# Linear attention that scales keys and queries by doubling block totals

## The chip, the cores and the metric

One core of one Trainium2 chip. The metric is device time in microseconds of one execution; less is better. The kernel computes two transformer blocks on 512 tokens of width 1024, in f32. Most products run on operands split in two fp32r parts (high and low), three products for one; the linear attention's inner products run on plain f32.

## The reference

Block 1 (two layers of feed-forward, pooling or convolution, feed-forward) and, in block 2, the softmax attention, the merge and the MLP are not touched. The change lies in block 2's gated linear attention: 4 heads, key width 128, value width 256, 512 tokens and 256 context tokens, run forward and backward. Cut to what matters:

```python
g = log_sigmoid(lowrank @ w_gk + b_gk) / 16            # per token and key channel, one for either direction
s_f = sum_t k_t * exp(b_last - b_t) v_t                # b = cumsum(g) over the context; s_b likewise, flipped
# in chunks of 64, state S from s_f:
b = cumsum(gc)
o_inter = (qc * exp(b)) @ state
a[i, j] = sum_d qc[i, d] kc[j, d] exp(b[i, d] - b[j, d])   for j <= i
o = o_inter + a @ vc
state = exp(b_last) * state + (kc * exp(b_last - b)).T @ vc
# the same on flipped time; the two outputs are added, normalized and gated
```

## The kernel before

Data lie transposed: channels on the 128 partitions, tokens along the free dimension. For one head H, `H.k` holds keys of 512 tokens and 256 context tokens, `H.q` the queries, `H.v` the values with tokens on partitions. The kernel works in chunks of 128 tokens.

The matrix of a chunk is built by halving. At level s (64, 32, ..., 1) a chunk falls in blocks of 2s tokens; each pair of a token in the left half and one in the right half of one block is decayed across the block's middle: the key by what lies from it to the middle, the query by what lies from the middle to it. In the right half's queries against the left half's keys this is the forward direction; in the left half's queries against the right half's keys the backward one. `masks` pick these pairs from a product of all keys and queries (`copy_predicated` into `H.A`), and the diagonal comes from undecayed keys and queries, times 2.

The decays come from TensorE. `decay` computes the log decays of 4 chunks (f32 products of the gate inputs `lr`, tokens as the stationary side, with `gkw`; then Abs, Exp, Ln, a VectorE step, and a split in Gh and Gl). For each direction there are 9 constant patterns of 128 x 128 (`pats`): a state's key, a state's query, and 7 levels. `gla_decays` multiplies two patterns at a time with Gl and Gh (L940, L941), and ScalarE takes the exponential of the sums into E (L942). `gla_level` multiplies halves of keys and queries by E into X and Y (L962), multiplies X by Y on TensorE (L966), and writes through the mask (L968). For the first pair of patterns `gla_states` instead scales keys (kd) and queries (qp), transposes the keys (`ktok`), and runs `state_step`: a product of transposed keys with values, and S times a chunk's total plus the product. `gla_ctx_keys` and `gla_ctx_states` do that for the context. `gla_final` adds the state's part in both directions and `H.A` times values.

The order: `gla_phase` goes through the heads. Between a head's pairs of patterns it places "fills": the next head's projections (keys, values, queries; after the last head the attention's keys), the head's two output gates, and some gates of the later merge; the next head's decays (`begin`) stand between them as well. The program order is only a priority: the framework's planner simulates the program with its own costs and gives every engine one fixed order, in which a ready instruction may pass one that isn't. Engines then run in that order and wait on semaphores. Weights come as 512 KB chunks over SyncE's queue into 3 raw slots; ScalarE casts each into a high part (L199), VectorE subtracts (L200), with 2 slots of either part. Sums in PSUM have 4 slots for this work ("mm") and 2 for projections ("pj").

The lines to follow: L204 to L206 are the three products of a projection, L871 to L873 those of the values, L782 the gate products, L838 the diagonal products, L879 the state products, L891 the transposes, L905 and L906 the context's pattern products.

Of the kernel before, what the change touches and what calls it, by code (L numbers as in the profile page):

```python
# [17 lines left out]
P = 128  # L18
# [14 lines left out]
LEVELS = (64, 32, 16, 8, 4, 2, 1)  # L33
NPAT = 2 + len(LEVELS)
GLA_FILLS = (0, 2, 1, 2, 3)
# [15 lines left out]
def consts():  # L51
# [10 lines left out]
    u = np.arange(P)[:, None]  # L62
    t = np.arange(P)[None, :]
    pats = np.zeros((2, NPAT, P, P), np.float32)
    masks = np.zeros((len(LEVELS), P, P), np.float32)
    for d in range(2):
        pats[d, 0] = (u > t) if d == 0 else (u < t)
        pats[d, 1] = (u <= t) if d == 0 else (u >= t)
        for n, s in enumerate(LEVELS):
            mid = (t // (2 * s)) * 2 * s + s  # L70
            left = t < mid
            if d == 0:
                key, query = (u > t) & (u < mid), (u >= mid) & (u <= t)
                pats[d, 2 + n] = np.where(left, key, query)
            else:
                query, key = (u >= t) & (u < mid), (u >= mid) & (u < t)
                pats[d, 2 + n] = np.where(left, query, key)
            j, i = u, t
            same = (j // (2 * s)) == (i // (2 * s))
            jl, il = (j % (2 * s)) < s, (i % (2 * s)) < s  # L80
            masks[n] = same & (jl != il)
    out["pats"] = np.ascontiguousarray(pats.transpose(2, 0, 1, 3) * GSCALE).reshape(P, 2 * NPAT * P).astype(np.float32)
# [18 lines left out]
def layout(inp):  # L101
# [47 lines left out]
    gw[0:16, 0], gw[64, 0] = a["w_gk_fwd_2"][0], a["b_gk_fwd_2"][0]  # L149
    gw[16:32, 1], gw[64, 1] = a["w_gk_bwd_2"][0], a["b_gk_bwd_2"][0]  # L150
# [15 lines left out]
class Builder:  # L166
# [165 lines left out]
    def out_rows(self, load, xs, gate, slots=()):  # L332
        """tail(seg, acc): x += gate * (W^T xs) and its sums of squares, the last rows by segments."""
# [326 lines left out]
    def gla_phase(self, ctx, gla):  # L660
# [3 lines left out]
        self.pe = self.pool(ctx, "glae", 1, reuse_waits="tile")  # L664
        self.pz = self.pool(ctx, "glaz", 2, reuse_waits="tile")
        self.lr = cp.tile([P, T + C], F32, name="lrT")
        nc.gpsimd.memset(self.lr, 1.0)
        H = self.gla_open(0, gla)
        self.first_values(H)
        npat = NPAT * P  # L670
        self.pats = [cp.tile([P, npat], F32R, name=f"pats{i}") for i in range(2)]
        for i in range(2):
            for s in range(0, npat, 576):
                raw = self.raw(d["pats"][:, i * npat + s:i * npat + s + 576], 576)
                nc.scalar.copy(self.pats[i][:, s:s + 576], raw)
# [4 lines left out]
        self.gkw = cp.tile([P, 2, 512], F32, name="gkw")  # L680
        nc.sync.dma_start(self.gkw, d["gkw"])
        self.eye2 = cp.tile([P, P], F32, name="eye2")
        nc.vector.tensor_scalar(self.eye2, self.ident, 2.0, None, ALU.mult)
        parts, begin = self.gla_proj(H), self.gla_begin(H)
        for step in (begin[0], parts[0], begin[1], parts[4], begin[3], begin[4]):
            step()
        for hd in range(GH):
            N = self.gla_open(hd + 1, gla) if hd + 1 < GH else None
            fills = self.gla_proj(N) if N else self.k_proj()
            fills += [lambda H=H, e=e: self.gla_gate(H, e) for e in range(2)]  # L690
            if hd == 0:
                fills += [lambda: self.merge_gates(1) for _ in range(1)]
            if not N:
                fills += [lambda: self.merge_gates(1) for i in range(3)]
            begin = self.gla_begin(N) if N else []
            self.gla_init(H)
            for n, p0 in enumerate(range(0, NPAT, 2)):
                E = self.gla_decays(H, p0)
                if n == 4 and N:
                    begin[4]()  # L700
                self.gla_level(H, p0, E)
                for f in fills[:GLA_FILLS[n]]:
                    f()
                fills = fills[GLA_FILLS[n]:]
                if N and n < 4:
                    begin[n]()
            self.gla_final(H)
            H = N

    def first_values(self, H):  # L710
        """The first head's values and, in the same products, the low-rank gate inputs of all heads."""
        nc = self.nc
        own = tuple(self.pe.tile([P, 1024], F32R, name=f"wv{i}", tag=f"E{i}", bufs=2) for i in range(2))
# [8 lines left out]
        for tts in ((4, 5), (0, 1), (2, 3)):  # L722
# [5 lines left out]
            nc.scalar.copy(self.lr[0:32, at:at + n], ps[0:32, :n])  # L728

    def gla_begin(self, H):  # L730
        H.G = [None, None]

        def direction(dr):
            H.G[dr] = self.decay(H.hd, [(dr, c * P) for c in range(4)])

        def context():
            H.Gc = self.decay(H.hd, [(b, T + c * P) for b in range(2) for c in range(2)])

        def states():
            direction(0)  # L740
            self.gla_ctx_states(H)

        return [context, lambda: self.gla_ctx_keys(H), lambda: None, states, lambda: direction(1)]
# [34 lines left out]
    def decay(self, hd, parts):  # L778
        nc = self.nc
        ps = self.psum()  # L780
        for n, (b, at) in enumerate(parts):
            nc.tensor.matmul(ps[:, n * P:(n + 1) * P], self.lr[:, at:at + P], self.gkw[:, b, hd * P:(hd + 1) * P],  # L782
                             start=True, stop=True)
        e = self.ptmp.tile([P, T], F32, name="ge", tag="sa")
        nc.scalar.activation(e, ps, AF.Abs)
        nc.scalar.activation(e, e, AF.Exp, scale=-1.0)
        nc.scalar.activation(e, e, AF.Ln, bias=1.0)
        nc.vector.scalar_tensor_tensor(e, ps, 0.0, e, ALU.min, ALU.subtract)
        hi = self.pz.tile([P, T], F32R, name="Gh", tag="Gh", bufs=3)
        lo = self.pz.tile([P, T], F32R, name="Gl", tag="Gl", bufs=3)  # L790
        self.split(hi, lo, e)
        return hi, lo

    def gla_open(self, hd, gla):
        H = SimpleNamespace(hd=hd, out=gla[2 * hd:2 * hd + 2])
        H.k = self.pk.tile([P, T + C], F32, name="kT", bufs=2)
# [4 lines left out]
    def gla_proj(self, H):  # L801
# [3 lines left out]
        def keys():  # L805
            w = self.wm(WM_G + 2 * H.hd)
            for xs, at, n in ((self.hcs, T, C), (self.hs, 0, T)):
                ps = self.psum("pj")
                self.proj(ps[:, :n], w, xs)
                nc.scalar.copy(H.k[:, at:at + n], ps[:, :n])  # L810
# [21 lines left out]
    def gla_init(self, H):  # L832
        nc = self.nc
        H.A = self.pz.tile([P, 4, P], F32, name="glaA", tag="glaA", bufs=2)
        ps = self.psum()
        for c in range(4):
            s = slice(c * P, (c + 1) * P)
            nc.tensor.matmul(ps[:, s], H.k[:, s], H.q[:, s], start=True, stop=True)  # L838
        nc.vector.tensor_tensor(H.A, ps.rearrange("p (c t) -> p c t", c=4), self.eye2.unsqueeze(1).to_broadcast([P, 4, P]), ALU.mult)
# [47 lines left out]
    def ktok(self, kd, n):  # L887
        nc = self.nc
        ps = self.psum()
        for c in range(n):  # L890
            nc.tensor.transpose(ps[:, c * P:(c + 1) * P], kd[:, c * P:(c + 1) * P], self.ident)  # L891
        kt = self.pz.tile([P, T], F32, name="ktok", tag="ktok")
        nc.scalar.copy(kt[:, :n * P], ps[:, :n * P])
        return kt

    def gla_ctx_keys(self, H):
        nc = self.nc
        gh, gl = H.Gc
        H.ctx = []
        for dr in range(2):  # L900
            ps = self.psum()
            for c in range(2):
                o = ps[:, c * 256:(c + 1) * 256]
                s = slice((dr * 2 + c) * P, (dr * 2 + c + 1) * P)
                nc.tensor.matmul(o, gl[:, s], self.pats[dr][:, 0:256], start=True, stop=False)  # L905
                nc.tensor.matmul(o, gh[:, s], self.pats[dr][:, 0:256], start=False, stop=True)  # L906
            E = self.pe.tile([P, 2, 2, P], F32, name="Ec", tag=f"E{dr}", bufs=2)
            nc.scalar.activation(E.rearrange("p c s t -> p (c s t)"), ps, AF.Exp)
            kd = self.pz.tile([P, T], F32, name="kd", tag="X")
            nc.vector.tensor_tensor(kd[:, :C].rearrange("p (c t) -> p c t", c=2), H.k[:, T:].rearrange("p (c t) -> p c t", c=2),  # L910
# [319 lines left out]
```

## Time and profile before

| what | value |
|---|---|
| timed runs, median of 3 | 2787.91 us (2782.96 to 2790.6) |
| the profiled execution, span | 2789.4 us (its own time is not given apart from the span) |
| TensorE products busy | 2749.3 us, 99% |
| VectorE, ScalarE, GpSimd busy | 1534.0, 973.7, 30.7 us |
| linear attention | about 1700 to 2054 us of the span |

Busy times add up what an engine's instructions cover. A product's own duration reaches to the end of its pipeline, so products overlap: their throughput is read from one start to the next. One f32 product on TensorE leaves two records, one in fp32r leaves one, a transpose one. What ended an idle time is inferred from semaphore events.

### The profile page before, as it was taken

To read this page: it belongs to the slowest core of one execution; us is meant where nothing else is said; L and a number is where in the kernel's file an instruction comes from. 1 tells how busy PE (TensorE), PEld (TensorE's weight loads), DVE (VectorE), ACT (ScalarE), POOL (GpSimd) and SP (SyncE) were. 2 spreads that over 40 slices of the span, in tenths; PEclk is the share of its full clock that TensorE was granted. 3 is DMA by queue.
4 is the path that set the end of the run, shared out by engine and by line. 5 is a ranking of instruction groups with operands and counts; after the bars stand their busy time and mean duration, and the time that the engine had idled before them with its cause. 6 is when DMAs were issued, how large, how long until landed. Compare 5 with 4: busy or idle time off the path is not lost.

```text
span 2789.4 us, 35584 instructions
## 1 busy us (share of the span) xinstructions
PE 2749.3 (99%) x14437; PEld 2374.9 (85%) x14437; DVE 1534.0 (55%) x2553; ACT 973.7 (35%) x1509; POOL 30.7 (1%) x39
## 2 busy tenths in 40 slices
PE   7999999999999999999999999999999999999999
PEld 6888889888898888988988889999898888888887
DVE  6645577444575446744865545455456665454443
ACT  4222244222242222322432234444456652333222
POOL 0000000000000000000000000000000000000000
PEclk9999999999999999999999999999999999999999
DMA  8745543444545455332455433111121134323332
GB/s 313 249 147 184 190 128 129 144 145 132 161 134 184 153 164 171 107 100 91 154 185 163 154 103 121 54 35 39 46 80 53 57 109 145 97 92 93 103 95 81
DMA packets 102980, 354.60 MB, mean 127 GB/s; under 512 B 11424, under 2 KB 11680, under 8 KB 102688
## 3 DMA queue, kind: packets, MB, share of 16 engines
q1 hardware_dynamic: 100800, 348.66, 39.5%
q10 hardware_dynamic: 2016, 3.67, 0.3%
q8 instruction: 113, 1.85, 0.3%
q14 instruction: 51, 0.42, 0.0%
HBM read 344.42 MB, written 7.86 MB: 126 GB/s over the span
## 4 chain that ended last, share of the span: by engine, by line
PE 96%; ACT 1%; DVE 1%; DMA 1%; issue 0%; POOL 0%; SPq 0%; DVEq 0%; ACTq 0%
PE mm L204 28%; PE mm L206 28%; PE mm L205 28%; PE mm L871 1%; PE mm L872 1%; PE mm L873 1%; PE mm L966 1%; PE mm L1078 1%; PE mm L879 1%; PE mm L941 1%; PE mm L940 1%; ACT whi L199 0%; PE mm L458 0%; PE mm L504 0%; PE nR L285 0%
## 5 line engine op out<-in xcount | busy, mean ns | idle before, releaser
L204 PE MATMUL mm<-hh,wlo 128*128 128x512 f32 (+1 forms) x2344 | 881.1, 378 | 2.8 <-ACT hh L301 1.8
L205 PE MATMUL mm<-hh,whi 128*128 128x512 f32 (+1 forms) x2344 | 878.9, 377 | 0.0
L206 PE MATMUL mm<-hl,whi 128*128 128x512 f32 (+1 forms) x2344 | 870.0, 377 | 0.4 <-DVE hl L302 0.3
L199 ACT CAST whi<-wraw 128x1024 fp32r<-128x1024 f32 (+1 forms) x443 | 457.0, 1034 | 904.8 <-PE mm L206 484.9
L200 DVE TENSOR_TENSOR wlo<-wraw,whi 128x1024 fp32r<-128x1024 f32 (+1 forms) x443 | 533.0, 1205 | 314.4 <-ACT whi L199 312.0
L204 PEld LDWEIGHTS mm<-hh,wlo 128*128 128x128 f32 x2344 | 442.8, 189 | 81.2 <-ACT hh L301 2.2
L205 PEld LDWEIGHTS mm<-hh,whi 128*128 128x128 f32 x2344 | 442.4, 189 | 77.6
L206 PEld LDWEIGHTS mm<-hl,whi 128*128 128x128 f32 x2344 | 437.5, 189 | 80.2 <-DVE hl L302 0.8
L205 PE MATMUL mm<-g,whi 128*128 128x512 f32 (+1 forms) x1147 | 416.2, 363 | 0.0
L204 PE MATMUL mm<-g,wlo 128*128 128x512 f32 (+1 forms) x1147 | 416.0, 363 | 0.0
L206 PE MATMUL mm<-g,whi 128*128 128x512 f32 (+1 forms) x1147 | 413.7, 362 | 0.0
L205 PEld LDWEIGHTS mm<-g,whi 128*128 128x128 f32 x1147 | 216.5, 189 | 33.5
L206 PEld LDWEIGHTS mm<-g,whi 128*128 128x128 f32 x1147 | 216.5, 189 | 33.5
L204 PEld LDWEIGHTS mm<-g,wlo 128*128 128x128 f32 x1147 | 216.5, 189 | 33.4
L249 DVE SCALAR_TENSOR_TENSOR adaw<-adaw,cond 128x1024 f32<-128x1024 f32 x176 | 208.7, 1220 | 2.5 <-DMA adaw<-in_ada_dram 2.5
L324 DVE SCALAR_TENSOR_TENSOR x<-mm,hg,x 128x512 f32<-128x512 f32 (+1 forms) x115 | 76.2, 662 | 186.2 <-PE mm L206 186.2
L363 DVE TENSOR_TENSOR gf<-sa,mm 128x512 f32<-128x512 f32 (+1 forms) x94 | 61.3, 653 | 200.4 <-PE mm L206 191.8
L362 ACT ACTIVATE sa<-mm 128x512 f32<-128x512 f32 (+1 forms) x94 | 53.6, 570 | 316.2 <-PE mm L206 316.2
L324 DVE SCALAR_TENSOR_TENSOR x<-mm,mod,x 128x512 f32<-128x512 f32 (+1 forms) x56 | 37.8, 674 | 134.1 <-PE mm L206 134.1
L301 ACT ACTIVATE hh<-hn,mod 128x256 fp32r<-128x256 f32 (+1 forms) x120 | 58.4, 519 | 58.5 <-DVE hn L300 49.5
L269 DVE TENSOR_TENSOR nacc<-nacc,sq 128x256 f32<-128x256 f32 (+1 forms) x108 | 52.2, 486 | 27.7 <-ACT sq L268 27.2
L268 ACT ACTIVATE sq<-x 128x256 f32<-128x256 f32 (+1 forms) x90 | 42.1, 468 | 67.7 <-DVE x L324 64.2
(283 smaller groups left out, 2812.7 us busy)
## 6 DMA issues: line engine op xcount, KB each, us to landing
wraw<-in_ffn_in_dram SPq DMA_DIRECT2D x176, 512.0 KB, 3.6
adaw<-in_ada_dram SPq DMA_DIRECT2D x176, 512.0 KB, 4.6
wraw<-in_wm_dram SPq DMA_DIRECT2D x66, 512.0 KB, 3.6
wraw<-in_mlp_dram SPq DMA_DIRECT2D x64, 512.0 KB, 3.9
wraw<-in_ffn_out_dram SPq DMA_DIRECT2D x64, 448.0 KB, 3.4
wraw<-in_ffn_out_dram SPq DMA_DIRECT2D x32, 512.0 KB, 3.6
wraw<-in_conv_in_dram SPq DMA_DIRECT2D x24, 512.0 KB, 3.5
ads<-in_ada_dram SPq DMA_DIRECT2D x8, 512.0 KB, 10.0
```

The costliest lines, as they stand in the source:

```text
L199: self.nc.scalar.copy(hi, src)
L200: return self.nc.vector.tensor_tensor(lo, src, hi.bitcast(F32), ALU.subtract)
L204: mm(ps, wlo, xhi, start=start, stop=False)
L205: mm(ps, whi, xhi, start=False, stop=False)
L206: mm(ps, whi, xlo, start=False, stop=stop)
L249: nc.vector.scalar_tensor_tensor(out, raw, 1.0, self.cond[:, cond], ALU.mult, ALU.mult, accum_out=dst)
L268: nc.scalar.activation(sq[:, :n], src, AF.Square, scale=g)
L269: nc.vector.tensor_tensor(acc, acc, sq[:, :n], ALU.add)
L301: nc.scalar.activation(hi, u, AF.Identity, bias=sh[:, k:k + 1])
L324: self.nc.vector.scalar_tensor_tensor(x, ps[:, :seg[1]], gate[:, k:k + 1], x, ALU.mult, ALU.add)
L362: nc.scalar.activation(sa, pa[:, :seg[1]], AF.Silu)
L363: nc.vector.tensor_tensor(gf, sa, pb[:, :seg[1]], ALU.mult)
```

## The change

The patterns, their products and their exponentials go, and with them the tiles E, Y, Gh and Gl. Decays now are products of decays. `H.tot` starts as each token's own decay in either direction (forward of context and tokens, backward of tokens and context; 1536 columns). Two stacked tiles, L = [context keys, keys, backward queries] and R = [forward queries, keys, context keys], hold keys and queries decayed to the borders of their block. One level with blocks of s tokens: X takes the left half-block keys of L and the right ones of R; the product with queries of both stacks (read with a two-step pattern from Z, which holds L and R) goes through the mask; then the left halves of L and the right halves of R are multiplied by the total of the other half, and totals are multiplied in pairs. Levels run from 1 to 64, each on the result of the one before; after the last, keys and queries are decayed to borders of a chunk, and the states follow (`gla_states`), now behind all levels, context included.

The gate: inputs, their remainders and the inputs again stand in rows 0 to 95 of `lr`, rounded to fp32r, the bias in rows 96 and 97; `gate_weights` prepares the stacked weights once (cast, remainder, cast, and two steps for rows 96 on). One product per direction and 512 columns then gives the gate. The number of fills and of merge gates is as before; their places between levels are new.

```diff
-LEVELS = (64, 32, 16, 8, 4, 2, 1)
+LEVELS = (1, 2, 4, 8, 16, 32, 64)
@@ gla_phase
-        self.pats = [cp.tile([P, npat], F32R, name=f"pats{i}") for i in range(2)]
-                raw = self.raw(d["pats"][:, i * npat + s:i * npat + s + 576], 576)
-                nc.scalar.copy(self.pats[i][:, s:s + 576], raw)
+        self.gate_weights(cp)
-        for step in (begin[0], parts[0], begin[1], parts[4], begin[3], begin[4]):
+        for step in (parts[0], lambda: self.gla_decay(H), parts[4], lambda: self.gla_enter(H)):
             step()
...
+                fills = [[p[0]], [p[4], lambda N=N: self.gla_decay(N)], [p[1]], [p[2]], [p[3], lambda N=N: self.gla_enter(N)]]
+                fills += [[g] for g in gates]
+            else:
+                fills = [[k[0]], [k[1]], [gates[0]], [gates[1]]] + [[m] for m in more]
+            for n in range(len(LEVELS)):
+                self.gla_level(H, n)
+                for f in fills[n]:
                     f()
+            self.gla_states(H)
             self.gla_final(H)
+    def gate_weights(self, cp):
+        self.gkw = cp.tile([P, 1024], F32R, name="gkw")
+        raw = self.raw(self.d["gkw"], 1024)
+        lo = self.wraw.tile([P, 1024], F32, name="gklo", tag="wraw")
+        hi = self.gkw.bitcast(F32)
+        nc.scalar.copy(self.gkw, raw)
+        nc.vector.tensor_tensor(lo[64:P], raw[64:P], hi[64:P], ALU.subtract)
+        nc.scalar.copy(self.gkw[64:96], lo[64:96])
+        nc.vector.tensor_scalar(raw[96:P], hi[96:P], self.ident[96:P, 96:97], None, ALU.mult)
+        nc.vector.scalar_tensor_tensor(self.gkw[96:P], lo[96:P], self.ident[96:P, 97:98], raw[96:P], ALU.mult, ALU.add)
@@ first_values, for each pair of token tiles
+            nc.scalar.copy(self.lr[0:32, s], ps[0:32, :n])
+            nc.vector.tensor_tensor(self.lr[32:64, s], ps[0:32, :n], self.lr[0:32, s].bitcast(F32), ALU.subtract)
+            nc.scalar.copy(self.lr[64:96, s], ps[0:32, :n])
+    def gla_decay(self, H):
+        groups = (((0, 0, T, C),), ((1, 0, T, T + C),), ((0, T, C, 0), (1, T, C, 2 * T + C)))
+        for group in groups:
+            for dr, t0, n, _ in group:
+                w = self.gkw[:, dr * T + H.hd * P:dr * T + (H.hd + 1) * P]
+                nc.tensor.matmul(ps[:, at:at + n], w, self.lr[:, t0:t0 + n], start=True, stop=True)
...
+        nc.scalar.activation(H.tot, H.tot, AF.Exp, scale=GSCALE)
+    def gla_enter(self, H):
+        nc.vector.tensor_tensor(H.L[:, T + C:], H.q, H.tot[:, T + C:2 * T + C], ALU.mult)
+        nc.vector.tensor_tensor(H.R[:, :T], H.q, H.tot[:, C:T + C], ALU.mult)
...
@@ keys of gla_proj
+                nc.scalar.copy(H.L[:, left:left + n], ps[:, :n])
+                nc.gpsimd.tensor_copy(H.R[:, right:right + n], H.L[:, left:left + n])
+    def gla_level(self, H, n):
+        nc.scalar.copy(blocks(X)[:, :, 0], blocks(H.L[:, C:C + T])[:, :, 0])
+        nc.scalar.copy(blocks(X)[:, :, 1], blocks(H.R[:, T:2 * T])[:, :, 1])
+        for c in range(4):
+            q = H.Z[:, T + C + c * P:T + C + (c + 1) * P]
+            dims = [[2 * s, P // (2 * s)], [T + s, 2], [1, s]]
+            q = bass.AP(q.tensor, q.offset, [list(q.ap[0])] + [x for x in dims if x[1] > 1])
+            nc.tensor.matmul(ps[:, t], X[:, t], q, start=True, stop=True)
+        nc.vector.copy_predicated(H.A, m, ps.rearrange("p (c t) -> p c t", c=4))
+        w = (2 * T + C) // s
+        for a, h, tot in ((H.L, 0, H.tot[:, :w]), (H.R, 1, H.tot[:, C // s:C // s + w])):
+            a = blocks(a)[:, :, h]
+            other = tot.rearrange("p (b h) -> p b h", h=2)[:, :, 1 - h]
+            nc.vector.tensor_tensor(a, a, other.unsqueeze(2).to_broadcast([P, w // 2, s]), ALU.mult)
+        pairs = H.tot.rearrange("p (b h) -> p b h", h=2)
+        nc.vector.tensor_tensor(H.tot, pairs[:, :, 0], pairs[:, :, 1], ALU.mult)   # a new tile
+    def gla_states(self, H):
+        kc = self.ktok([L[:, :P], L[:, P:C], R[:, 2 * T:2 * T + P], R[:, 2 * T + P:]])
+        kts = [self.ktok([a[:, c * P:(c + 1) * P] for c in range(4)]) for a in (L[:, C:C + T], R[:, T:2 * T])]
...
+        H.qp = [R[:, :T], L[:, T + C:]]
```

## Rows read from the trace of the kernel before

**Rows 1.** The page, parts 1 and 2: busy time of each engine; granted clock of 40 slices.
```profile
PE 2749.3 (99%) x14437; PEld 2374.9 (85%) x14437; DVE 1534.0 (55%) x2553; ACT 973.7 (35%) x1509; POOL 30.7 (1%) x39
...
PEclk9999999999999999999999999999999999999999
```

**Rows 2.** Busy time by stretch: stretch, us, then each engine's busy us (instructions).
```profile
1690.00:1740.00 50.00, 46.38 (x335) 43.82 (x334) 28.73 (x64) 27.11 (x60) 1.06 (x2) 1.00 0.47 152
...
sum 370.00, PE 362.63 PEld 334.12 DVE 182.19 ACT 167.89 POOL 4.08; mean PE 72.53 PEld 66.82 DVE 36.44 ACT 33.58 POOL 0.82
```

**Rows 3.** What TensorE waited for, 1690 to 2060 us: total, times, longest.
```profile
PE mm L966 <- DVE X L962: 2.6, 2, 1.6
...
PE mm L879 <- ACT ktok L893: 0.7, 3, 0.2
```

**Rows 4.** Groups by line and shape, TensorE, 1690 to 2065: count | busy, mean ns | idle.
```profile
L940 PE MATMUL mm<-pats,Gl 128*128 128x256 f32 x128 | 33.7, 295 | 0.1
...
L966 PE MATMUL mm<-Y,X 128*128 128x128 f32 x224 | 27.9, 276 | 2.6 <-DVE X L962 2.6
...
L782 PE MATMUL mm<-gkw,lrT 128*128 128x128 f32 x96 | 12.8, 276 | 0.0
...
L940 PE MATMUL mm<-pats,Gl 128*128 128x128 f32 x32 | 7.3, 273 | 0.0
...
L905 PE MATMUL mm<-pats,Gl 128*128 128x256 f32 x16 | 4.7, 309 | 0.0
```

**Rows 5.** Timeline of TensorE, 1747 to 1761: start us, us, instruction.
```profile
1747.60 0.39 PE L204 MATMUL mm<-hh,wlo 128*128 128x512 f32 x1
...
1749.86 0.39 PE L205 MATMUL mm<-hh,whi 128*128 128x512 f32 x1
...
1759.67 0.28 PE L940 MATMUL mm<-pats,Gl 128*128 128x256 f32 x1
...
1760.62 0.28 PE L873 MATMUL mm<-wlo,hc 128*128 128x256 f32 x1
```

**Rows 6.** Timeline, 2037 to 2045, around a level's products in head 3.
```profile
2043.46 1.06 PE L966 MATMUL mm<-Y,X 128*128 128x128 f32 x8
...
2044.27 0.48 PE L206 MATMUL mm<-hl,whi 128*128 128x512 f32 x1
...
2044.56 0.74 DVE L968 COPY_PREDICATED glaA<-masks,mm 128x512 f32<-128x512 uint8 x1 [5.48 <-PE mm L966]
2044.59 0.40 PE L204 MATMUL mm<-hh,wlo 128*128 128x512 f32 x1
```

**Rows 7.** Line L838, the diagonal products: duration ns, first and last start.
```profile
L838 PE MATMUL mm<-qT,kT x32: 273/275/275, 1757.2 to 1977.6; 128*128 128x128 f32 x32
```

**Rows 8.** Groups by line and shape, VectorE, 1690 to 2065.
```profile
L200 DVE TENSOR_TENSOR wlo<-wraw,whi 128x1024 fp32r<-128x1024 f32 x31 | 37.9, 1223 | 47.3 <-ACT whi L199 47.1
L962 DVE TENSOR_TENSOR X<-kT,E 128x256 f32<-128x256 f32 x56 | 23.6, 421 | 27.2 <-ACT E L942 27.1
...
L968 DVE COPY_PREDICATED glaA<-masks,mm 128x512 f32<-128x512 uint8 x28 | 20.6, 736 | 25.5 <-PE mm L966 25.0
L884 DVE SCALAR_TENSOR_TENSOR S<-S,E,mm 128x256 f32<-128x256 f32 x24 | 10.9, 480 | 10.5 <-PE mm L879 10.2
...
L977 DVE TENSOR_TENSOR kd<-kT,E 128x512 f32<-128x512 f32 x8 | 5.5, 688 | 2.5 <-ACT E L942 2.5
```

**Rows 9.** Line L962, the half multiplies: duration ns min/median/max.
```profile
L962 DVE TENSOR_TENSOR X<-kT,E x56: 415/420/428, 1778.6 to 2038.7; 128x256 f32<-128x256 f32 x56
```

**Rows 10.** Groups by line and shape, ScalarE, 1690 to 2065.
```profile
L942 ACT ACTIVATE E<-mm 128x512 f32<-128x512 f32 x72 | 40.3, 598 | 30.0 <-PE mm L941 22.6 <-issue 7.0
L199 ACT CAST whi<-wraw 128x1024 fp32r<-128x1024 f32 x31 | 32.4, 1044 | 2.4 <-PE mm L872 2.4
...
L268 ACT ACTIVATE sq<-x 128x256 f32<-128x256 f32 x5 | 2.1, 414 | 3.1 <-DVE x L324 2.1 <-DVE nacc L269 1.0
```

**Rows 11.** Groups by line and shape, GpSimd, the whole span.
```profile
L280 POOL TENSOR_TENSOR nr<-nm,mhalf 128x4 f32<-128x4 f32 x5 | 6.0, 1194 | 359.1 <-DVE nm L279 359.1
```

More of the change, by code (lines that the diff above doesn't have):

```diff
@@ L61, in consts @@
     out["band"] = band
-    u = np.arange(P)[:, None]
-    t = np.arange(P)[None, :]
-    pats = np.zeros((2, NPAT, P, P), np.float32)
+    j = np.arange(P)[:, None]
+    i = np.arange(P)[None, :]
     masks = np.zeros((len(LEVELS), P, P), np.float32)
[L66 to L82, printed above, removed]
+    for n, s in enumerate(LEVELS):
+        masks[n] = ((j // (2 * s)) == (i // (2 * s))) & ((j % (2 * s) < s) != (i % (2 * s) < s))
     out["masks"] = np.ascontiguousarray(masks.transpose(1, 0, 2))
@@ L688, in gla_phase @@
             N = self.gla_open(hd + 1, gla) if hd + 1 < GH else None
-            fills = self.gla_proj(N) if N else self.k_proj()
-            fills += [lambda H=H, e=e: self.gla_gate(H, e) for e in range(2)]
-            if hd == 0:
[L692 to L702, printed above, removed]
-                    f()
-                fills = fills[GLA_FILLS[n]:]
-                if N and n < 4:
-                    begin[n]()
+            gates = [lambda H=H, e=e: self.gla_gate(H, e) for e in range(2)]
@@ new lines, in gla_phase @@
+            if N:
+                p = self.gla_proj(N)
+                fills = [[p[0]], [p[4], lambda N=N: self.gla_decay(N)], [p[1]], [p[2]], [p[3], lambda N=N: self.gla_enter(N)]]
+                fills += [[g] for g in gates]
+            else:
+                k = self.k_proj()
+                more = [lambda: self.merge_gates(1) for _ in range(3)]
+                fills = [[k[0]], [k[1]], [gates[0]], [gates[1]]] + [[m] for m in more]
+            if hd == 0:
+                fills[-1].append(lambda: self.merge_gates(1))
@@ L710, in first_values @@
     def first_values(self, H):
         nc = self.nc
-        own = tuple(self.pe.tile([P, 1024], F32R, name=f"wv{i}", tag=f"E{i}", bufs=2) for i in range(2))
+        own = tuple(self.pz.tile([P, 1024], F32R, name=f"wv{i}", tag=f"wv{i}", bufs=1) for i in range(2))
         wv = [self.chunk(self.d["wv0"][:, 3 * VW * i:min(3 * VW * (i + 1), KT * VW)], min(3, KT - 3 * i) * VW,
@@ L727, in first_values @@
                 nc.tensor.transpose(ps[0:32, i * P:(i + 1) * P], lt[:, tt], self.ident)
[L728 to L743, printed above, removed]
+            s = slice(at, at + n)
+            nc.scalar.copy(self.lr[0:32, s], ps[0:32, :n])
+            nc.vector.tensor_tensor(self.lr[32:64, s], ps[0:32, :n], self.lr[0:32, s].bitcast(F32), ALU.subtract)
+            nc.scalar.copy(self.lr[64:96, s], ps[0:32, :n])
     def k_proj(self):
@@ L806, in keys @@
             w = self.wm(WM_G + 2 * H.hd)
-            for xs, at, n in ((self.hcs, T, C), (self.hs, 0, T)):
+            for xs, left, right, n in ((self.hcs, 0, 2 * T, C), (self.hs, C, T, T)):
                 ps = self.psum("pj")
                 self.proj(ps[:, :n], w, xs)
-                nc.scalar.copy(H.k[:, at:at + n], ps[:, :n])
+                nc.scalar.copy(H.L[:, left:left + n], ps[:, :n])
+                nc.gpsimd.tensor_copy(H.R[:, right:right + n], H.L[:, left:left + n])
         def queries():
@@ L885, in state_step, with ktok @@
         return Sn
-    def ktok(self, kd, n):
+    def ktok(self, parts):
         nc = self.nc
         ps = self.psum()
[L890 to L893, printed above, removed]
-        return kt
[L896 to L910, printed above, removed]
-                                    E[:, :, 0], ALU.mult)
-            edge = P - 1 if dr == 0 else 0
-            tot = self.psmall.tile([P, 2], F32, name="ctot")
-            nc.vector.tensor_copy(tot, E[:, :, 1, edge])
-            H.ctx.append((self.ktok(kd, 2), tot))
@@ L993, in attention_phase @@
+        kt = self.pz.tile([P, T], F32, name="ktok", tag="ktok", bufs=3)
+        nc.scalar.copy(kt, ps)
+        return kt
     def attention_phase(self, ctx):
```

153 lines of the change are left out of this document (52 added, 101 removed).

## The prediction

> **What bounds the kernel now.** I read the page's busy times first: TensorE is busy 99% of the span at the full granted clock, 2.4 GHz in all 40 slices; VectorE stands at 55%, ScalarE at 35% [rows 1]. So a microsecond of matrix work that goes is worth close to a microsecond, wherever it stands, and other engines' work counts only where it makes TensorE wait. Next the table by stretch, over the linear attention (1690 to 2060 us): TensorE 362.6 of 370 us, so 7.4 us idle, with VectorE busy 182 and ScalarE 168, half their time [rows 2]. TensorE's own waits there: the level products waited 2.6 us for their scaled keys and the state products 0.7 us for transposed keys [rows 3]; the rest of the 7.4 lies ahead of head 0, which the change hardly touches. The planner threads the chain of a head (decays, levels, states) between projections so well that only throughput counts. The question is whether it still can.
>
> **Prices on TensorE.** Busy times of products overlap, so I price from start to start. Ten 512-column products take 2.26 us, 0.226 each; eight 256-column ones 0.95 us, 0.119 each [rows 5]. A 128-column f32 product is two records; four of them, from 2043.46 to the start of the second product after them, take 1.13 us less the 0.23 of the one between: 0.90, or 0.112 per record [rows 6]. I price a 128-column fp32r record the same.
>
> **Removed from TensorE.** The pattern products: 256 of 256 columns in the levels (L940 shown, 128, and L941 as many), 64 of 128 columns (32 on either line), 32 of 256 for the context (16 on L905 and as many on L906) [rows 4]. That is 288 x 0.119 = 34.3 plus 64 x 0.112 = 7.2, together 41.5 us. The gate products: 96 records [rows 4] x 0.112 = 10.7 us; in their place 4 heads x (2 of 512 and 2 of 256 columns), 8 x 0.226 + 8 x 0.119 = 2.8 us. Net 7.9. Total removed: **49.4 us**. The same before and after: 28 x 4 level products, the diagonal products, 12 transposes and 10 state products per head, the final products, all projections and gates.
>
> **VectorE and ScalarE.** VectorE loses the 112 half multiplies of the levels (47.2), the splits of the log decays, and the multiplies for kd and qp and the context, some 71 us. It gains 56 multiplies of 640 elements. Between 256 (0.421) and 512 (0.688) an element costs 1.04 ns [rows 8], so 640 cost 0.82: 46 us. To these come the products of block totals, 2.7 us per head (768 elements down to 12), 8 entry multiplies of 0.69, and 5 us for the stacked rows: 67 us. Nothing is won or lost. ScalarE loses 72 exponentials (40.3 busy) [rows 10] and 15 us of smaller work, and gains 56 copies of 256 elements at 0.41, 23 us, and 9 us of decay and gate weights. Both have room. GpSimd's copies of the keys (8) have no row of their kind; the nearest is 1.19 us for a four-column power [rows 11]. I take 1 us, with ends 0.3 and 4. They lie beside decays and queries, which must come first, so they cost nothing; at 4 us head 0 might wait 2.
>
> **The chain of a head, the new part.** Before, all 9 patterns of a head could be evaluated ahead of use. Now a level waits for the one ahead of it: two copies into X on ScalarE (0.82), eight records on TensorE (1.06 to the end [rows 6]), then on VectorE the masked write (0.74) and two multiplies (1.64) [rows 8], and about 0.2 of handing over (2043.46 + 1.06 ends 0.04 ahead of the masked write [rows 6]): 4.5 us, of which 0.9 is TensorE's own. Seven levels: 31.5 us, 6.3 of them TensorE's, so some 25 us have to be covered by other products. The covers are the fills: per head keys 24 x (0.226 + 0.119) = 8.3, queries 5.4, values 144 x 0.119 = 17.1, two gates 10.8: 41.6 us; the last head has 43.7 (attention keys, gates, three merge gates). Each of the seven slots holds at least 5.4. From first to last diagonal product three heads took 220.4 us [rows 7], 73.5 each; without 12.4 they are 61, against 31.5 of levels and about 11 of states and outputs, nearly all of the latter TensorE's own. So I expect cover to suffice, by 16 us a head, less what queues.
>
> What queues: ScalarE and VectorE work in order, and a chain instruction can stand behind a weight split (1.05 on ScalarE, 1.22 on VectorE) [rows 8, 10] and a fill's evacuation (0.6). If half of these 2.9 us hits each level, cover needed rises by 10 us a head to 35: still under 41.6.
>
> **What I add.** Waits of TensorE in the level chain: nothing to 37 us (worked out below); before it was 2.6, I take 5. End of each head: the states now come last, so first copy of transposed keys (0.6) and last state step (0.48) may show, 0 to 2 us each, I take 1, together 4. The handover to attention, where tiles of its keys come to lie over tiles that now live to the last output: 0 to 10, I take 2, since query and value products stand ready. Start of head 0: the pattern loads and casts go, the preparation of gate weights (two casts and three multiplies, 5 us in a row) comes, both under 20 us of value products: 0, with ends -1 and +6. The old 3.3 goes [rows 3].
>
> Sum on the profiled execution: 2789.4 - 49.4 - 3.3 + 5 + 4 + 2 = 2747.7. It has its span alone; that is 1.5 above the median of the timed runs (2787.9), so I carry that over: **2746**.
>
> **One rule against it.** In the first two levels (blocks of 1 and 2) the moving operand alternates between two regions 4 KB apart after each element or two. The halves that VectorE multiplied were strided as well, with blocks from 64 down to 1, and their times lie between 415 and 428 ns [rows 9]; nothing in them depends on the block. No row shows TensorE reading like that. 32 products (64 records) would be affected. A record takes 0.112 where 128 columns of the 512-column rate are 0.057, so the stream may become twice as slow before it shows; at four times it costs 0.115 x 64 = 7 us, and the time would be 2753. The Trainium skill (SBUF — State Buffer, section "Door 1: The DMA port swizzle") says that SBUF is read in lines of 16 bytes, that full bandwidth needs at least two hits per line, and that each step to a new line is charged; by that rule these two levels read badly. The trace can't decide it.
>
> **Rivals.**
> 1. The chain shows through. If all 2.9 us of a split and an evacuation, and 0.8 of totals and misjudged order, hit every level, 25 + 26 = 51 us need cover where 41.6 stand: 9.3 a head, 37 in all; this gives 2746 + 37 - 5 = 2778. For it: one instruction late in program order holds TensorE, whose order is fixed by the planner's own costs. Against: both engines idle half the time, and before the change the same planner left 3.3 us.
> 2. Slower than before: the same place, but gates' three ScalarE passes (0.6 each) queue too. Each level is then late by d; TensorE loses (25 + 7d - 41.6) x 4. That eats the 49.4 (and the 5 + 4 + 2 beside them) from d = 4 us on; at d = 4.9 (a split, three passes and a 0.74 multiply all in front, each time) the loss is 70 and the time 2746 - 5 + 70 = 2811. Against: no row shows a level waiting that long; the largest wait was 1.6 of the 2.6 [rows 3].
> 3. The 7 us of strided reads: 2753, by the rule above.
> 4. The change doesn't do what it says, since the removed products filled gaps that stay: then the idle time would grow by what went. Against: TensorE was never short of ready products in that stretch. It would give about 2785.
>
> **How the numbers follow.** Forecast 0.70, rival 1 0.13, rival 2 0.05, rival 3 0.08, rival 4 0.04. About 0.3%, 8.4 us, can be told from no change. Faster by more, under 2779.5: forecast, rival 3, and most of rival 1: 0.90. Same: what is left of rival 1 and most of rival 4: 0.05. Slower: 0.05. Range: low end with no added wait and the fastest of the runs' scatter (5 under the median): 2747.7 - 11 - 5, about 2732; the high end takes in rival 3, the handover's 10 and head 0's 6, and two thirds of rival 1: 2770.
>
> **What would show it.** Right: no instruction on pattern or Ec lines, 320 + 32 products less, TensorE's busy time about 49 lower, the level products' waits under 10 us in all, diagonal products about 61 us apart from head to head, other stages as long as before. Wrong: TensorE idle beside VectorE's multiplies of L and R, or beside X copies that stand behind weight casts; level products of blocks 1 and 2 longer than those of 4 to 64; a hole at the start of attention. A total within 8 us of before would mean that the chain, and no longer TensorE, sets the pace.

## The result and the profile after

The changed kernel takes 2805.14 us (median of 4, 2802.12 to 2807.56) beside 2788.2 of the kernel before: a ratio of 1.0063, 95% interval 1.0046 to 1.008. It is slower by 17 us where 42 us less were forecast. The profiled execution has a span of 2801.0 us.

The page after, answering to [rows 1]: TensorE's busy time and records, then the granted clock of 40 slices.

```profile
PE 2740.1 (98%) x14005; PEld 2329.8 (83%) x14005; DVE 1531.2 (55%) x2499; ACT 949.7 (34%) x1474; POOL 35.2 (1%) x47
...
PEclk9999999999999999999999998999999999999999
```

The records are 432 fewer, which is 352 patterns and 96 old gate products less 16 new ones, as counted. But busy time fell by 9.2 us instead of 49, although the records went. Something that stayed got longer. The prediction had "other stages as long as before" as a check, and that is the check that fails. By 1709 us (start of the last norm of block 1; 1686.8 before) the changed kernel is already 22.6 us late, and TensorE has run no product of the linear attention by then.

So compare the same work in an early stage of both: one uninterrupted series of 336 products with the normed tiles (hh, hl) moving. First and last product, start and duration, in the kernel before, then in the changed kernel:

```profile
561.20 0.39 PE L204 MATMUL mm<-hh,wlo 128*128 128x512 f32 x1
...
637.13 0.39 PE L206 MATMUL mm<-hl,whi 128*128 128x512 f32 x1
```

```profile
520.46 0.40 PE L187 MATMUL mm<-g,wlo 128*128 128x512 f32 x1
...
563.80 0.39 PE L189 MATMUL mm<-g,whi 128*128 128x512 f32 x1
564.03 0.40 PE L187 MATMUL mm<-hh,wlo 128*128 128x512 f32 x1
...
642.19 0.39 PE L189 MATMUL mm<-hl,whi 128*128 128x512 f32 x1
```

75.93 us over 335 steps is 0.2267 each before; 78.16 is 0.2333 after. The series with the hidden tiles (g) moving ahead of it is 192 products long: 43.34 us over 191 steps, 0.2269, as before (43.29, 0.2266). Both run at the full granted clock, with no wait. There are 6120 products of the slower kind in the kernel; at 0.0060 to 0.0066 each (mean over all stages 0.2270 and 0.2330) that is 37 to 40 us.

Inside the linear attention, what TensorE waited for, 1690 to 2100 us: total, times, longest. It answers to [rows 3].

```profile
PE mm L910 <- ACT wv L182: 9.0, 1, 9.0
PE mm L847 <- ACT X L840: 7.2, 3, 2.6
PE fR L268 <- POOL fr L631: 4.2, 1, 4.2
PE mm L918 <- ACT ktok L932: 2.3, 3, 1.3
PE fsum L256 <- DVE nacc L252: 2.3, 1, 2.3
PE nsum L256 <- DVE nacc L252: 1.9, 2, 1.4
PE go L889 <- DVE S L923: 1.7, 1, 1.7
```

The level chain (L847) waits 7.2 us in three waits out of 28 levels; the largest wait stands ahead of head 0, where values wait for a weight cast. In that hole the clock falls, and the first products behind it run at the lower level (1.2 GHz). TensorE's busy time (and instructions) and granted clock by stretch, first around the hole, then directly behind it, then the sum of the table that answers to [rows 2]:

```profile
1730.00:1747.00 17.00, 2.35 (x13) 0.60 0.17 63
1747.00:1764.00 17.00, 16.80 (x114) 0.90 0.12 31
...
1746.90:1750.30 3.40, 3.40 (x14) 0.50 0.50 124
1750.50:1753.90 3.40, 3.40 (x28) 1.00 0.03 11
...
sum 390.00, PE 360.69 PEld 329.43 DVE 200.19 ACT 166.39 POOL 13.55; mean PE 72.14 PEld 65.89 DVE 40.04 ACT 33.28 POOL 2.71
```

TensorE is idle for 29 us of 390 instead of 7.4 of 370. Diagonal products, answering to [rows 7], lie 55.3 us apart from head to head (73.5 before, 61 forecast). They stand earlier in the next head than forecast, so this says nothing of a loss. The sums of the heads' output norms say more: they lie 69.0 us apart, 75.7 before, so a head got 6.7 us shorter where 12.4 were forecast.

```profile
L784 PE MATMUL mm<-qT,Z x32: 271/275/275, 1781.6 to 1947.5; 128*128 128x128 f32 x32
```

### The profile page after: what moved, and what is told of

Read it like the earlier page. It is cut to its first block, busy times and chain, and to the rows that moved or that the text cites. A ratio compares the mean times of both kernels' runs of the same rounds, so it can differ in the third digit from the quotient of the medians.

```text
span 2801.0 us, 34594 instructions
## 1 busy us (share of the span) xinstructions
PE 2740.1 (98%) x14005; PEld 2329.8 (83%) x14005; DVE 1531.2 (55%) x2499; ACT 949.7 (34%) x1474; POOL 35.2 (1%) x47
## 4 chain that ended last, share of the span: by engine, by line
PE 95%; ACT 2%; DVE 1%; DMA 1%; issue 0%; POOL 0%; SPq 0%; DVEq 0%; ACTq 0%
PE mm L187 29%; PE mm L189 29%; PE mm L188 29%; PE mm L910 1%; PE mm L847 1%; PE mm L911 1%; PE mm L912 1%; PE mm L1021 1%; ACT whi L182 1%; PE mm L918 1%; PE nR L268 0%; PE mm L441 0%; PE mm L487 0%; PE sc L1005 0%; PE mm L474 0%
## 5 line engine op out<-in xcount | busy, mean ns | idle before, releaser
L187 PE MATMUL mm<-hh,wlo 128*128 128x512 f32 (+1 forms) x2344 | 890.9, 382 | 2.8 <-ACT hh L284 1.9
L188 PE MATMUL mm<-hh,whi 128*128 128x512 f32 (+1 forms) x2344 | 888.3, 381 | 0.0
L189 PE MATMUL mm<-hl,whi 128*128 128x512 f32 (+1 forms) x2344 | 879.4, 381 | 0.4 <-DVE hl L285 0.3
L1103 DVE TENSOR_TENSOR rl<-rl 128x512 f32<-128x512 f32 (+1 forms) x36 | 22.5, 632 | 79.2 <-ACT rl L1102 79.0
```

The costliest lines, as they stand in the source:

```text
L187: mm(ps, wlo, xhi, start=start, stop=False)
L188: mm(ps, whi, xhi, start=False, stop=False)
L189: mm(ps, whi, xlo, start=False, stop=stop)
```

## Where each microsecond went: the theories

**PLACE.** The removed `gla_ctx_states` held a small tile, `ctot` (4 buffers of 32 bytes), in a pool that is laid out once for the whole kernel. Without it, every tile allocated later, weights and hidden tiles among them, stands 128 bytes lower, while the normed tiles, allocated earlier, stay. By the program's tile addresses the weights lie at a multiple of 512 bytes from the normed tiles before, and at 384 modulo 512 after. Theory: the rate of a product depends on that distance. Rival: something in the new code or its data traffic slows everything.

**HANDOVER.** The last part of head 0's values (the third chunk, tiles `wv`) got its high and low parts in a pool whose range reaches over block 1's scratch tiles (before, they lay in the pool of the exponentials, which did not). Theory: for that reason the planner placed its cast behind the whole final norm. On ScalarE's and TensorE's timeline of the changed kernel, start and duration, with the idle time ahead in brackets:

```profile
1735.56 1.01 POOL L631 TENSOR_TENSOR fr<-fm,mhalf 128x4 f32<-128x4 f32 x1 [22.95 <-DVE fm L630]
...
1736.62 1.22 PE L268 MATMUL fR<-ident,fr 128*128 128x128 f32 x4 [4.16 <-POOL fr L631]
...
1743.95 0.91 ACT L284 ACTIVATE hh<-hn,mod 128x256 fp32r<-128x256 f32 x2 [0.94 <-DVE hn L283]
...
1744.87 1.28 ACT L570 ACT_TABLE_LOAD   x1
1746.17 0.67 ACT L182 CAST wv<-wraw 128x576 fp32r<-128x576 f32 x1
...
1746.89 0.61 PE L910 MATMUL mm<-wv,hc 128*128 128x288 f32 x1 [9.04 <-ACT wv L182]
```

The cast is short (0.67), but stands last in ScalarE's order. Before, it ran at 1703.03, in the middle of the norm (the line below). Two of the new gate-weight operations may lengthen the hole as well: on VectorE they stand at 1731.66 (0.75) and 1733.36 (1.28), while the norm's sums, done at 1732.46, are first used at 1734.67. No run moves these two alone.

```profile
1703.03 0.66 ACT L199 CAST wv<-wraw 128x576 fp32r<-128x576 f32 x1
```

**SWITCH.** From one head to the next `gla_final` takes both PSUM slots "pj" for its norm, so the next projection cannot start. Before, the next head's transposes (L891) and state products (L879), which use slots "mm", ran in that gap, between the norm's sums (L273) and its product nR (L285); its pattern products stood just ahead of the sums. TensorE in the kernel before, at the switch after head 0:

```profile
1832.77 1.01 PE L273 MATMUL nsum<-ones,nacc 128*128 128x1 f32 x8
...
1833.95 0.64 PE L891 MATMUL mm<-ident,kd 128*128 128x128 f32 x4
...
1835.26 1.99 PE L879 MATMUL mm<-gv,ktok 128*128 128x256 f32 x8 [0.24 <-ACT ktok L893]
1837.09 1.05 PE L285 MATMUL nR<-ident,nr 128*128 128x128 f32 x8
```

The change moves these behind all levels, so in the gap only the next head's level chain is left, and it is too short of cover there. **CHAIN**, its rival: the chain of a level is too long wherever it stands. The switch after head 0 in the changed kernel, TensorE, VectorE, ScalarE and GpSimd:

```profile
1851.72 0.70 PE L256 MATMUL nsum<-ones,nacc 128*128 128x1 f32 x5
...
1851.82 0.72 DVE L849 COPY_PREDICATED glaA<-masks,mm 128x512 f32<-128x512 uint8 x1
...
1852.44 1.54 DVE L854 TENSOR_TENSOR Z<-Z,tot 128x640 f32<-128x640 f32 x2
...
1854.20 1.01 POOL L263 TENSOR_TENSOR nr<-nm,mhalf 128x4 f32<-128x4 f32 x1 [64.66 <-DVE nm L262]
...
1854.52 0.41 ACT L840 COPY X<-Z 128x256 f32<-128x256 f32 x1
...
1854.99 1.16 PE L847 MATMUL mm<-Z,X 128*128 128x128 f32 x8 [2.57 <-ACT X L840]
...
1855.98 1.72 PE L268 MATMUL nR<-ident,nr 128*128 128x128 f32 x8
...
1857.35 0.56 PE L187 MATMUL mm<-hc,wlo 128*128 128x256 f32 x1
```

TensorE has nothing between the sums (1852.4) and 1854.99; the projection of keys comes only at 1857.35, and the 256-column products then start 0.21 us apart until 1859.4 and 0.12 after: the granted clock is 0.50, the lower level, from 1856.4 to 1859.5, and 1.00 behind that. Before, it was 1.00 in this stage.

## The experiments

**PLACE, given back and taken away.** An unused tile of 128 bytes is added to the changed kernel; and in the kernel before, `ctot` moves to a pool that lives only in the linear attention, nothing else changed.

```diff
+        nc.vector.memset(self.psmall.tile([P, 32], F32, name="pad", bufs=1), 0.0)
```

> The kernel after the change with one unused tile of 128 bytes per partition put into the pool of small tiles, so that everything allocated behind it (weights, g) lies again at the addresses relative to h that it had before; nothing else is changed. Theory PLACE (the removed ctot tiles, 4 x 32 bytes, moved the weights by 128 bytes against hh and hl, and products that read both run at 0.233 us in place of 0.227): the 512-column products with hh or hl moving go back to 0.227 in every stage; 6100 of them x 6.4 ns = 39 us; time 2805 - 39 = 2766 (2758 to 2775). Theory ORDER (the slow rate in block 1 is not of addresses, and the loss is the chain of the heads and the handover alone): rate stays 0.233, time 2805 within 5.

Measured: 2770.61 (2766.01 to 2771.15), ratio to before 0.9934 [0.9916, 0.9951]. Waits in the linear attention as in the changed kernel. The same 336 products:

```profile
555.70 0.39 PE L187 MATMUL mm<-hh,wlo 128*128 128x512 f32 x1
...
631.64 0.39 PE L189 MATMUL mm<-hl,whi 128*128 128x512 f32 x1
```

75.94 us, 0.2267 again. TensorE's busy time is 2705.0, so 44.3 below before.

```diff
-            tot = self.psmall.tile([P, 2], F32, name="ctot")
+            tot = self.pz.tile([P, 2], F32, name="ctot", bufs=4)
```

> The kernel before with the four ctot tiles moved from the pool of small tiles to the pool of the linear attention, so that weights lie 128 bytes lower against hh and hl, as after the change; same instructions. PLACE: products with hh or hl moving slow down from 0.227 to 0.233 everywhere, those with g stay; time 2788 + 39 = 2827 (2818 to 2836). ORDER: 2788 within 5.

Measured: 2821.86 (2820.09 to 2825.88), ratio 1.0123 [1.0101, 1.0144], the series at 0.2333. The kernel before, with its old computation, gets 34 us slower when one small tile moves to another pool. The rival falls: nothing of the new code is in it.

**Half the distance.** Filler of 64 bytes instead of 128, so 448 modulo 512.

> The kernel after the change with 64 bytes of filler instead of 128: weights 64 bytes below their old distance from h. PLACE says only that the distance decides; it doesn't say how. If any odd distance is bad, 0.233 and 2805; if the cost grows with the distance, about 0.230 and 2785; if lines of 64 bytes count, 0.227 and 2766. ORDER: 2805 within 5.

Measured: 2780.77 (2778.59 to 2784.84), ratio 0.9977 [0.9967, 0.9987]; mean step 0.2291. In between, nearest to a cost that grows with the distance; the next two runs overturn that.

**Which distances.** Two runs of the changed kernel with block 1's weights in five named slots, each moved by its own number of bytes; only the rates are read.

```diff
+            o, c = self.offs[i] // 4, "ABCDE"[i]
+            slots = tuple(p.tile([P, 1152], F32R, name=f"{t}{c}", tag=f"{t}{c}", bufs=1)[:, o:o + 1024] for p, t in ((self.whi, "whi"), (self.wlo, "wlo")))
```

> The kernel after the change with block 1's ten weight slots (high and low, A to E) shifted one by one, by 32, 64, 96, 160 and 192 bytes inside larger tiles (two raw slots in place of four to make room, so the total time says little). Against hh and hl the distances mod 512 are 416, 448, 480, 32 and 64; against g they are 32, 64, 96, 160 and 192. PLACE: the time from start to start of 512-column products differs between slots A to E, for one slot it differs between hh and g, and it is 0.227 for none but a distance near 0. ORDER: all slots have one rate.

> The changed kernel with the weight slots of block 1 moved by 224, 256, 288, 352 and 448 bytes from where they stood, one slot each; only the start-to-start times of 512-column products by slot are read. The distance to the normed tiles, modulo 512, becomes 96, 128, 160, 224 and 320; to the hidden tiles (moved with the weights, distance 0) 224, 256, 288, 352 and 448. PLACE with one good distance only: 0.2265 at none of them, 0.2290 at 448, 0.2333 at the others unless they repeat with 256 (then 0.2265 at 256 and 0.2290 at 192 plus or minus 256).

Measured in one run of each, us from start to start, means of some 270 to 1550 consecutive products (good to about 0.0001); every slot gives two distances, one to the hidden tiles (its shift) and one to the normed tiles (384 more):

```
distance mod 512   0      32     64     96     160    192    224    256    288    352    448
hidden (g)         0.2268 0.2332 0.2332 0.2337 0.2338 0.2294 0.2334 0.2275 0.2329 0.2342 0.2291
distance mod 512   32     64     96     128    160    224    320    384    416    448    480
normed (hh, hl)    0.2331 0.2334 0.2339 0.2334 0.2335 0.2334 0.2333 0.2328 0.2331 0.2290 0.2333
```

Slot B of the second run shows it with one set of weights: the first and last of 24 products each, normed tiles moving (distance 128), then hidden tiles (distance 256).

```profile
66.57 0.40 PE L192 MATMUL mm<-hh,wloB 128*128 128x512 f32 x1
...
71.94 0.39 PE L194 MATMUL mm<-hl,whiB 128*128 128x512 f32 x1
...
150.37 0.39 PE L192 MATMUL mm<-g,wloB 128*128 128x512 f32 x1
...
155.58 0.40 PE L194 MATMUL mm<-g,whiB 128*128 128x512 f32 x1
```

0.2335 and 0.2265. Only 0 and 256 are fast, 192 and 448 lie in between, all others tried are slow (0.2328 to 0.2342): a repeat with 256 bytes fits every cell. "One good distance only" fell. The cost does not grow with distance: 32 bytes off is as bad as 128.

**HANDOVER alone** (with the filler): the third chunk's tiles in the pool of keys and values, whose range ends below block 1's scratch tiles (it lies over block 1's weights and hidden tiles instead).

```diff
-        own = tuple(self.pz.tile([P, 1024], F32R, name=f"wv{i}", tag=f"wv{i}", bufs=1) for i in range(2))
+        own = tuple(self.pk.tile([P, 1024], F32R, name=f"wv{i}", tag=f"wv{i}", bufs=1) for i in range(2))
```

> The 128-byte filler as in e1 (2771), and the two tiles that take the third chunk of the first value weights come from another pool, glak, in whose place no tile of block 1's norm lay; after the change they lay in glaz, which reaches over that norm's temporaries, and the planner put the cast behind the whole norm. Theory HANDOVER: the 9.0 us wait on that cast goes, the clock doesn't fall to 1.2 GHz there (17 us), and the time falls by 9 + 3 to 12: 2758 to 2763. Theory HEADS ONLY (TensorE has nothing to do there anyway until the norm is done, since the values read the same norm's output): the wait moves to the norm, 2769 to 2773.

Measured: 2760.99 (2754.96 to 2761.27), ratio 0.9893 [0.9877, 0.991]; 9.6 less. The cast runs at 1701.4 and L910's wait is 2.6 us, now for normed tiles; the granted clock is 1.00 around it (1680 to 1748).

**SWITCH and CHAIN, one edit each** (with the filler alone). First the masked write behind the two multiplies, which takes 0.74 us out of every level's chain from multiply to multiply. As the edit shows, it stands ahead of the product of totals, not behind it as the expectation says:

```diff
-        nc.vector.copy_predicated(H.A, m, ps.rearrange("p (c t) -> p c t", c=4))
...
+        nc.vector.copy_predicated(H.A, m, ps.rearrange("p (c t) -> p c t", c=4))
         nc.vector.tensor_tensor(H.tot, pairs[:, :, 0], pairs[:, :, 1], ALU.mult)
```

> e1 with the masked write of a level placed behind the two multiplies and the product of totals, which takes 0.73 us out of the chain from level to level. Theory CHAIN (my rival: the seven dependent levels are too long for the fills): 28 x up to 0.7 us less waiting, above all the 7.2 us of waits for X; 2771 - 5 to 10 = 2761 to 2766. Theory SWITCH (the waits stand at the change from head to head, where no projection is ready): the chain is not what binds, 2768 to 2771.

Measured: 2769.46 (2768.57 to 2769.68), 0.9929 [0.9915, 0.9944]: nothing beyond the filler. Then the norm of every head in the slots "mm":

```diff
-        R = self.norm_rows(acc, 4, 2 * P, "pj" if H.hd < GH - 1 else "mm")
+        R = self.norm_rows(acc, 4, 2 * P, "mm")
```

> e1 with the output norm's two sums of heads 0 to 2 in the PSUM slots 'mm' instead of the two slots 'pj', which the next head's projections need. SWITCH: in the kernel after, a norm holds both slots for some 7 us at the end of a head, and no projection can start; before the change the next head's pattern products, in 'mm', ran there. Projections now fill the place: the waits of the level products for X (7.2 us in all) and the dips of the clock there go, 2771 - 10 to 15 = 2756 to 2761. CHAIN: the waits come back at later levels, 2768 to 2773.

Measured: 2770.41 (2768.01 to 2770.97), 0.9932 [0.9917, 0.9947]: nothing either, a miss for SWITCH. (What ran in the gap before were transposes and state products, as the rows above show, not pattern products.) Its waits, 1670 to 2110 us:

```profile
...
PE mm L930 <- DVE Z L854: 4.8, 3, 1.6
...
PE go L889 <- DVE S L923: 3.1, 4, 1.4
PE mm L847 <- ACT X L840: 2.7, 1, 2.7
```

The level products' waits went from 7.2 to 2.7, as SWITCH wanted, but the transposes (L930), which had no wait in the changed kernel, now wait 4.8 us for the last multiplies (L854), which stand behind the last level's masked write in VectorE's order, and final products 3.1 for states. The gap moved from the head's start to the end of its chain. If that is so, the late mask, which shortens that chain, should be worth something only together with this edit.

**All three edits.**

> e1 with all three edits (third chunk early, masked write late, norm sums in 'mm'). If HANDOVER and SWITCH hold, their gains add: 2771 - 10 - 12 = 2749, and TensorE's waits in the linear attention are under 10 us; this would be the 2746 of my forecast. If they only hide each other: 2758 to 2765.

Measured: **2749.4** (2747.08 to 2753.03), ratio 0.9859 [0.9845, 0.9874], faster than both kernels. The page, then the largest waits, 1670 to 2110 us:

```profile
PE 2700.3 (98%) x14005; PEld 2324.9 (85%) x14005; DVE 1531.3 (56%) x2500; ACT 947.3 (34%) x1474; POOL 35.0 (1%) x47
```

```profile
PE go L889 <- DVE S L923: 3.1, 4, 1.4
PE mm L910 <- DVE hl L285: 2.6, 2, 1.6
PE mm L847 <- ACT X L840: 2.5, 3, 2.2
...
PE mm L930 <- DVE Z L852: 1.0, 1, 1.0
```

TensorE's busy time is 49.0 us below before: the number that was forecast for it.

The two kinds of loss at the switches, waiting and clock, both shrink against HANDOVER alone. There the granted clock was 0.98, 0.95 and 0.98 over 1800 to 1870, 1870 to 1940 and 1940 to 2010 us; with all three edits it is 1.00, 1.00 and 0.98. How the gain splits between the two wasn't tested.

**Pairs, to see whether the last 11.6 us are one edit's.** Both with filler and the third chunk's tiles moved: the late mask without the norm edit, and the norm edit without the late mask.

> The version with the filler, the third chunk's tiles in the earlier pool and the masked write behind the multiplies and totals; the norm sums stay in the projections' PSUM slots. Before: 2788. With filler and earlier chunk alone 2761.0, with all three edits 2749.4. JOINT (the last 11.6 us need both the freed projection slots and the shorter chain, since either alone gained 0 to 1): 2758 to 2762, level products still wait 6 to 7 us for X. LATE ALONE (the late mask gives most of it once the handover is mended): 2749 to 2754, level products' waits under 4 us.

> The version with the filler, the third chunk's tiles in the earlier pool and the norm sums of all heads in the mm slots; the masked write stays ahead of the multiplies. JOINT: 2758 to 2762, with waits of transposes for the multiplies' last result (about 5 us) and of the output products for states (about 3) as with the norm edit alone. NORM ALONE (freed projection slots give it all once the handover is mended): 2749 to 2753, transposes wait under 2 us.

Measured: 2756.93 (2755.39 to 2761.98), 0.9905 [0.9891, 0.992], X waits 6.6; and 2761.67 (2755.01 to 2763.99), 0.9915 [0.99, 0.9931], with waits of 4.8 (L930) and 3.1 (L889). Neither is distinguishable from 0.9893 without them, and both lie above all three edits' interval: JOINT holds. (The first median is 1 us under JOINT's range, and 4 under HANDOVER alone; with this scatter that may be nothing, or a small part of the 11.6 that the late mask gives alone.)

**All three edits without the filler.**

> All three edits but without the 128-byte filler, so weights stand 384 bytes (modulo 512) from the normed tiles again. PLACE as a rate of every product with the normed tiles moving, independent of the waits: 2749.4 + 34.5 = 2784 (2779 to 2789), start to start 0.2333 us. If part of the place's cost was only waits that these edits remove: 2760 to 2775, at the same rate.

Measured: 2785.71 (2785.35 to 2790.97), ratio 1.0 [0.9991, 1.001], mean step 0.2330: 36.3 more than with it. The place costs the same beside few waits as beside many. By it alone a change that is worth 39 us reads as no change at all.

## Why the prediction was wrong, point by point

- **What the sum started from: the step that failed.** The sum took 2789.4 and changed only terms of the linear attention; "other stages as long as before" stood as a check, and no term had a price for it. They became 34 to 36 us longer (2805.14 less 2770.61; 2785.71 less 2749.4), since removing `ctot` moved the weights against the normed tiles. No row of before shows it, because there every such distance is fast. The diff did: a tile in a pool of the whole kernel goes. I read the diff for instructions and not for tiles.
- **Removed from TensorE, 49.4: right.** Records 432 fewer as counted; with the place restored, busy time is 44.3 to 49.0 lower, and 49.0 in the version with all three edits.
- **Start of head 0, 0 with ends -1 and +6: mis-sized.** 9.6 us. I priced the gate weights' five operations, not where the value tiles lie. What was late was a 0.67 us cast in ScalarE's order, through the pool that its tiles were given; moving the tiles alone takes the 9.6 away. The clock added to the hole: 14 products in 3.4 us at a granted clock of 0.50, 28 in the next 3.4 us at 1.00, so about 1.7 us (an estimate from these two rows).
- **Waits of the level chain, 5, and ends of heads, 4: together 11.6 beyond what the mended version still has.** Within a head 7 fills do cover the chain, as worked out: of 28 levels three waited. The gap opens between heads, where I had put only the copy and the last state step. The waits by themselves came out near their terms: 7.2 for 5, and for the ends 2.3 (L918) and 1.7 (L889), 4.0 for 4. What had no term is the clock behind the gaps: at the first switch 3.1 us at a granted clock of 0.50, about 1.6 us lost (an estimate), and the same dip stands behind the other two. Rival 4 came nearest, with another size and other products: what had filled the gap at the switch, transposes and state products, wasn't removed but moved behind the levels. Rival 1's queueing at every level did not occur. Rival 2 has the right sign and the wrong mechanism: no level was late by 4 us.
- **Handover to attention, 2:** no wait there is larger than 1.4 (the norm's sums). From the last output product to the first attention score it is 29.1 us (2062.9 to 2092.0) where it was 26.5; that fits the 2, and the version with all three edits still has 28.9; it was not tested by itself.
- **VectorE neutral, ScalarE some 23 less: right** (1531.2 and 949.7 against 1534.0 and 973.7).
- **Strided reads, rival 3: the mechanism is there, the price is a quarter.** Level products of head 0 in the version with all three edits at the full granted clock, levels 1, 2 and 4, each with the product after it:

```profile
1750.20 1.48 PE L847 MATMUL mm<-Z,X 128*128 128x128 f32 x8
1751.37 0.53 PE L188 MATMUL mm<-hh,whi 128*128 128x512 f32 x1
...
1756.16 1.12 PE L847 MATMUL mm<-Z,X 128*128 128x128 f32 x8
1757.03 0.96 PE L765 MATMUL mm<-lrT,gkw 128*128 128x512 f32 x4
...
1762.10 1.05 PE L847 MATMUL mm<-Z,X 128*128 128x128 f32 x8
1762.91 0.36 PE L910 MATMUL mm<-whi,hl 128*128 128x256 f32 x1
```

To the next start it is 1.17, 0.87 and 0.81 us, within 0.01 in all four heads: 0.36 and 0.06 more for blocks of 1 and 2, in four heads 1.7 us, not 7. (The regions lie 513 and 514 columns apart, 2 KB; the prediction's 4 KB was an error.) The Trainium skill (SBUF — State Buffer, section "Door 1: The DMA port swizzle") says that full bandwidth needs at least two hits per 16-byte line and that each step to a new line pays a penalty. The trace agrees in its order: one value per visit costs 0.36 us, two 0.06, four nothing seen.

- **The range.** Its high end, 2770, doesn't hold all that it names: 2746 with 7 for rival 3, 8 more for the handover, 6 for head 0 and two thirds of rival 1's 32 is about 2788. Even that lies below what was measured, since no term stood for the place.

Together: 2746 + 34.5 + 9.6 + 11.6 = 2801.7, 3.4 below the measured 2805.14; the same 3.4 separates 2746 from 2749.4. The three terms are differences from one run to the next, so they close by construction and the sum proves nothing more; that 2749.4 lies so near 2746 is partly luck, since its terms were not each as forecast (strided reads cost 1.7 us that the sum had at nothing).

What stays open: why the distance matters. The runs show on what it depends, not what in the chip does it. How the 9.6 and the 11.6 split in waiting and clock is estimated above and was not tested.

## What to carry to other kernels

Before comparing two versions, compare a stage that the change doesn't touch, product by product: if its rate differs, the difference is in layout and not in the change. When a change adds or removes a small tile in a long-lived pool, look at the addresses of everything allocated after it. And when work that was "cheap filler" goes or moves, look for the places where nothing else was ready (here the PSUM slots between heads), and expect that two mends may be worth nothing one by one.

## What the runs showed of the hardware

- A 512-column product with new weights each time takes 0.227 us from start to start where the byte distance of weights and moving tile is 0 modulo 256, 0.229 where it is 192 modulo 256, and 0.233 to 0.234 at every other distance tried (multiples of 32). Over 6120 such products a step from the first to the last cost 34 to 36 us of 2800.
- After a stretch of 17 us with TensorE busy for 2.35 (granted clock 0.60 over it) the next 17 us had a mean granted clock of 0.90: 14 products took the 3.4 us in which 28 ran right after. So a hole can cost more than its length. A wait of 2.6 us at a switch, behind eight one-column products, was followed by 3.1 us at the lower level (1.2 GHz, granted clock 0.50) too.
